# A small triangular inversion moved among the projections of r and v, affine steps on ScalarE, fillers given out anew

## The chip, the cores and the metric

One core of a Trainium2 chip runs one launch. The metric is the device time of that launch in microseconds (us). TensorE (PE) multiplies matrices, VectorE (DVE) and ScalarE (ACT) work elementwise, GpSimd (POOL) takes a few steps, and SyncE (SP) issues the loads.

## What is computed

Two layers over 256 positions of width 1024. A layer is a mixer and a feed-forward part (PEER), each followed by a LayerNorm. The mixer projects its input once, to the inputs of three branches and of their gates; the branches are a gated linear recurrence (RG-LRU), RWKV-7 and attention with low-rank latents (MLA). The change lies in the mixer, for the most part in RWKV-7:

```python
r, k, v, xw, xa, xg = split_last(p, (RW_WIDTH, RW_WIDTH, RW_WIDTH, LORA_W, LORA_A, LORA_G))
w = -jax.nn.softplus(-(w0 + jnp.tanh(xw) @ w2)) - 0.5
a = jax.nn.sigmoid(a0 + xa @ a2)
...
kk = hd(k * k_k).astype(jnp.float32)
kk = kk / jnp.maximum(jnp.sqrt(jnp.sum(kk * kk, -1, keepdims=True)), 1e-12)
k = k * (1.0 + (a - 1.0) * k_a)
decay = jnp.exp(-jnp.exp(w.astype(jnp.float32)))
...
xs = (tm(f32h(r)), tm(f32h(decay)), tm(f32h(k)), tm(f32h(v)), tm(-kk), tm(kk * a_h))
def step(state, inp):
    r_t, w_t, k_t, v_t, aa_t, bb_t = inp
    sa = jnp.einsum('bhvk,bhk->bhv', state, aa_t)
    state = (state * w_t[:, :, None, :] + sa[..., None] * bb_t[:, :, None, :]
             + v_t[..., None] * k_t[:, :, None, :])
    return state, jnp.einsum('bhvk,bhk->bhv', state, r_t)
```

The recurrence over 256 steps is computed in four chunks of 64 positions. In a chunk the delta rule needs the inverse of a triangular 64x64 matrix per head, whose entries are products of `kk` and `kk * a` with their decays. So there are 4 chunks x 8 heads = 32 such matrices in a layer.

## The kernel before, in words

**Projections.** All matrices are multiplied in a split form: `stream()` loads a 128x1024 weight tile (L82), ScalarE rounds it to `hi` (L84), VectorE subtracts to get `lo` (L88), and `projecting()` issues 24 matmuls for it (L247 to L249: hi times x-hi, hi times x-lo, lo times x-hi). It is a generator that yields every three matmuls, a *piece*. Each tile so needs one `lo` of VectorE before its third matmul.

**Fillers.** `rwkv_prep()` and `rwkv_scan()` are the main line. Beside them stands a list of generators: the latents and attention scores of MLA (`lat`), the projections of RG-LRU (`rgp`, `rgg`), the gates of branch 1 and the output products of branches 2 and 0. `fill(n, r)` takes n pieces from the front of that list, and before them up to r steps of the generator `rg_scan()`, once its inputs are there. Where the `fill` calls stand in the program, and with what n, sets what runs beside the main line; the scheduler then orders each engine's instructions by it.

**`rwkv_prep()`** projects the LoRA inputs and k, computes `at` and `sg` (L471 to L476), the head norms, then projects r and v, four tiles each with `fill(4)` behind each. After that come the gate, for layer 1 the value residual, the scan of the decays (`cum`, L542), its exponentials (L545 to L547), and two tiles per chunk, `AR` (with `kk` and r) and `KB` (with k and `kk * a`), L559 to L565. One set of matmuls per chunk gives all products of `KB` and `AR`; VectorE masks them into `GM` (L582).

**`rwkv_scan()`** inverts. POOL copies the diagonal 32x32 blocks of the triangles out of `GM` (`lu`, L602), VectorE transposes them (`lt`, L605) and runs 31 steps of substitution on all 64 blocks at once, a product (L613) and a sum (L615) each, each dependent on the one before: 62 instructions. L617 to L629 lay the result out (`tts`, `tp`, `t1s`, `t1u`, `TT`). `fill(124, 5)` stands behind as cover. Then TensorE joins the 32x32 blocks to 64x64 ones: eight groups of L638, which read `t1u`, eight more of L647, each with `fill(2)`. Then follows the scan over four chunks, in each four groups of small matmuls with `fill(4, 3)`, `fill(5, 3)` and `fill(2, 3)` between, and the group norm (L712). L310 in `head_bcast()` copies head statistics for a transposition, L463 scales k, L474 adds w0, L495 is an affine step of `at`, L729 the first tap of the convolution.

Of the kernel before, what the change touches and what calls it, by code (L numbers as in the profile page):

```python
# [45 lines left out]
def trunk(ctx, tc, x, xT, w_in, w_br, w_out, w_q, skT, uT, vt, prm, lora, g2, v1, v2, rgw, w_uq, w_ukv,  # L46
# [232 lines left out]
    def mixer(l, mp):  # L279
# [172 lines left out]
        def rwkv_prep():  # L452
            nonlocal la, k_, at, sg, r_, v_, g_, GM, VS, KS, AR, KB, pcm
# [29 lines left out]
            r_ = c4("r")  # L483
            for i in range(4):
                shifted(T_R + i, r_[:, i, :])
                fill(4)
            for b in range(2):
                V.tensor_mul(kk[:, :, b * P:(b + 1) * P], kk[:, :, b * P:(b + 1) * P], head_bcast(rs, b))
            v_ = c4("v")
            for i in range(4):  # L490
                shifted(T_V + i, v_[:, i, :])
                fill(4)
            t2 = c4("t2")
            for i in range(4):
                V.tensor_scalar(t2[:, i, :], at[:, i, :], ka[:, l, i:i + 1], ka[:, l, 4 + i:5 + i], op0=OP.mult, op1=OP.add)  # L495
# [42 lines left out]
            rmask = mp.tile([P, 1024], F32, tag="yt", name=nm("rmask"))
            G.memset(rmask, 1.0)
            G.memset(rmask[:, 0:1024:64], 0.0)  # L540
            cum, e1 = c4("t1"), c4("t2")
            V.tensor_tensor_scan(cum.rearrange("p i t -> p (i t)"), rmask,  # L542
                                 sg.rearrange("p i t -> p (i t)"), 0.0, op0=OP.mult, op1=OP.add)
            V.tensor_sub(sg, cum, sg)
            A.activation(e1, cum, AF.Exp, scale=-EXPM)  # L545
            A.activation(cum, cum, AF.Exp, scale=EXPM)
            A.activation(sg, sg, AF.Exp, scale=-EXPM)  # L547
            pcm = mp.tile([P, 4, 4, 2], F32, tag="pcm", name=nm("pcm"))
            e4 = e1.rearrange("p i (c t) -> p i c t", c=4)
            V.tensor_mul(pcm, e4[:, :, :, 63:64].to_broadcast([P, 4, 4, 2]),  # L550
                         bones[:, None, None, :].to_broadcast([P, 4, 4, 2]))
            AR = mp.tile([P, 4, 4, 2, 64], F32, tag="AR", name=nm("AR"))
            KB = mp.tile([P, 4, 4, 2, 64], F32, tag="KB", name=nm("KB"))

            def ch(t):
                return t.rearrange("p i (c t) -> p i c t", c=4)

            for i in range(4):
                V.tensor_mul(AR[:, i, :, 0, :], ch(kk)[:, i], ch(sg)[:, i])  # L559
# [647 lines left out]
```

## Time and profile before

| | us |
|---|---|
| Median of 3 runs | 2335.33 (2332.97 to 2336.89) |
| The profiled execution, its own time | 2339.72 |
| Its span in the profile | 2338.0 |
| TensorE busy in the span | 2242.7 |
| VectorE busy | 1790.2 |
| ScalarE busy | 1088.5 |
| GpSimd busy | 278.4 |

The profile's times count from the span's start. The mixer of layer 0 lies at about 10 to 345 us, that of layer 1 at about 1175 to 1510 us. Busy time of TensorE counts a matmul at half clock as twice as long, so a busy engine isn't one at its best; the granted clock stands beside it as a share of 2.4 GHz.

### The profile page before, as it was taken

Reading aid. Unit: us, or ns where it says so; the run is one execution under the profiler, and the core shown is the slowest. Engines: PE = TensorE matmul, PEld = TensorE weight load, DVE = VectorE, ACT = ScalarE, POOL = GpSimd, SP = SyncE. Lnnn points to the kernel's source line nnn. Section 1 sums busy time; section 2 is a strip of 40 time slices with the busy share of each in tenths; the row PEclk is TensorE's granted clock in tenths of the full one; section 3 lists DMA queues with packets and bytes.
Section 4 is the critical chain, followed back from the end, with each engine's and each line's share of the span. In section 5 each row is a group of like instructions: output and inputs, shape, how many; then the busy total and the mean of one; then the engine's idle time right before and its main releaser. Section 6 shows DMA issues by size and latency. Waiting matters only on the chain. (4 is left out here: it accounts for less than half of the span.)

```text
span 2338.0 us, 39856 instructions
## 1 busy us (share of the span) xinstructions
PE 2242.7 (96%) x15748; PEld 1980.1 (85%) x15748; DVE 1790.2 (77%) x3268; ACT 1088.5 (47%) x1635; POOL 278.4 (12%) x220
## 2 busy tenths in 40 slices
PE   7999989999999999999899999899999999999998
PEld 6888879998888888888787888799988888888886
DVE  6777877966788888755666877789668888887556
ACT  4543534445555544444445534344455555444443
POOL 0010016930000000000000100179300000000000
PEclk9998999999999999999999989999999999999999
DMA  6323344555555555655552234445555555556554
GB/s 212 118 79 113 133 164 146 165 184 185 175 170 172 173 176 170 213 196 190 189 174 91 91 109 134 160 142 170 183 184 177 172 171 172 174 171 214 194 193 136
DMA packets 104925, 381.88 MB, mean 163 GB/s; under 512 B 11649, under 2 KB 12161, under 8 KB 104481
## 3 DMA queue, kind: packets, MB, share of 16 engines
q1 hardware_dynamic: 104736, 379.32, 48.7%
q8 instruction: 124, 2.03, 0.3%
q14 instruction: 65, 0.52, 0.1%
HBM read 374.56 MB, written 4.72 MB: 162 GB/s over the span
## 5 line engine op out<-in xcount | busy, mean ns | idle before, releaser
L84 ACT CAST hi<-raw 128x1024 fp32r<-128x1024 f32 x658 | 690.3, 1050 | 756.2 <-PE acc L262 343.7
L88 DVE TENSOR_TENSOR lo<-raw,hi 128x1024 fp32r<-128x1024 f32 x570 | 696.0, 1222 | 250.0 <-ACT hi L84 242.5
L262 PE MATMUL acc<-hi,a 128*128 128x512 f32 x2000 | 554.6, 392 | 0.9 <-ACT a L166 0.9
L247 PE MATMUL mm<-xt,hi 128*128 128x256 f32 x1760 | 516.3, 294 | 23.7 <-ACT hi L84 11.7
L249 PE MATMUL mm<-xt,lo 128*128 128x256 f32 x1760 | 508.5, 290 | 13.9 <-DVE lo L88 10.5
L248 PE MATMUL mm<-xt,hi 128*128 128x256 f32 x1760 | 507.5, 288 | 0.0
L994 PE MATMUL acc<-xt,hi 128*128 128x512 f32 x1344 | 474.4, 399 | 0.0
L262 PEld LDWEIGHTS acc<-hi,a 128*128 128x128 f32 x2000 | 370.9, 188 | 76.2 <-ACT a L166 1.2
L247 PEld LDWEIGHTS mm<-xt,hi 128*128 128x128 f32 x1760 | 345.3, 196 | 31.0 <-ACT hi L84 11.7
L249 PEld LDWEIGHTS mm<-xt,lo 128*128 128x128 f32 x1760 | 344.3, 196 | 20.1 <-DVE lo L88 12.5
L997 PE MATMUL acc<-xt,lo 128*128 128x256 f32 x1344 | 348.7, 280 | 0.0
L248 PEld LDWEIGHTS mm<-xt,hi 128*128 128x128 f32 x1760 | 345.4, 196 | 2.1 <-issue 0.8
L262 PE MATMUL acc<-lo,a 128*128 128x512 f32 x1000 | 311.4, 391 | 0.0
L994 PEld LDWEIGHTS acc<-xt,hi 128*128 128x128 f32 x1344 | 245.4, 188 | 44.4
L88 POOL TENSOR_TENSOR lo<-raw,hi 128x512 fp32r<-128x512 f32 x176 | 251.5, 1455 | 244.9 <-ACT hi L84 243.2
L997 PEld LDWEIGHTS acc<-xt,lo 128*128 128x128 f32 x1344 | 253.5, 189 | 12.1
L262 PEld LDWEIGHTS acc<-lo,a 128*128 128x128 f32 x1000 | 187.7, 188 | 40.6 <-DVE lo L88 0.2
L1002 ACT COPY H<-acc 128x256 f32<-128x256 f32 x168 | 62.7, 373 | 232.0 <-PE acc L994 232.0
L1003 DVE TENSOR_TENSOR H<-H,acc 128x256 f32<-128x256 f32 x168 | 70.1, 417 | 60.8 <-ACT H L1002 60.8
L167 DVE SCALAR_TENSOR_TENSOR a<-H,a 128x1024 fp32r<-128x1024 f32 x64 | 78.4, 1225 | 44.7 <-ACT a L166 44.7
L166 ACT ACTIVATE a<-H 128x1024 fp32r<-128x1024 f32 x64 | 67.9, 1060 | 77.2 <-PE acc L262 76.9
L1094 DVE SCALAR_TENSOR_TENSOR H<-sm,H 128x512 f32<-128x512 f32 x128 | 87.7, 685 | 19.4 <-PE sm L1091 18.6
(356 smaller groups left out, 2381.4 us busy)
## 6 DMA issues: line engine op xcount, KB each, us to landing
raw<-in_uT_dram SPq DMA_DIRECT2D x256, 512.0 KB, 3.5
raw<-in_vt_dram SPq DMA_DIRECT2D x256, 512.0 KB, 3.8
raw<-in_w_in_dram SPq DMA_DIRECT2D x100, 512.0 KB, 3.5
raw<-in_w_q_dram SPq DMA_DIRECT2D x32, 512.0 KB, 3.5
raw<-in_w_br_dram SPq DMA_DIRECT2D x24, 512.0 KB, 3.6
raw<-in_w_out_dram SPq DMA_DIRECT2D x16, 512.0 KB, 4.1
ln<-in_lnp_dram SPq DMA_DIRECT2D x8, 512.0 KB, 4.9
xd<-ln SPq DMA_DIRECT2D x6, 512.0 KB, 2.6
```

The costliest lines, as they stand in the source:

```text
L84: A.copy(hi, raw)
L88: eng.tensor_sub(lo[:, c:c + n], raw[:, c:c + n], hi[:, c:c + n].bitcast(F32))
L166: A.activation(hi, src, AF.Copy, scale=scale)
L167: V.scalar_tensor_tensor(lo, src, scale, hi.bitcast(F32), op0=OP.mult, op1=OP.subtract)
L247: T.matmul(pt, h3[:, k, :], xth[:, k, :], start=(k == 0), stop=False)
L248: T.matmul(pt, h3[:, k, :], xtl[:, k, :], start=False, stop=False)
L249: T.matmul(pt, l3[:, k, :], xth[:, k, :], start=False, stop=(k == 7))
L262: T.matmul(acc[b][hf], m[:, bs], w[:, 512 * hf:512 * hf + 512], start=(k == 0 and j == 0), stop=(k == n - 1 and j == 2))
L994: T.matmul(p, h3[:, k, :], xt[:, k].rearrange("p a t -> p (a t)"), start=(k == 0), stop=(k == 7))
L997: T.matmul(p[:, 0:S], l3[:, k, :], xt[:, k, 0], start=False, stop=False)
L1003: V.tensor_add(h, h, p[:, 0:S])
L1094: V.scalar_tensor_tensor(hv, p.rearrange("p (t e) -> p e t", t=8), 1 / GATE_SCALE, hv, op0=OP.mult, op1=OP.mult)
```

## The change

- A new generator `ahead()` in `rwkv_prep()` holds the preparation of the decays, the halves of `AR` and `KB` that need neither r nor v, and the whole inversion. It makes the triangles by 32 small matmuls of its own (L530, 64x64) and 16 masked products (L535, 32x4x32) in place of the eight copies L602. It is stepped three times per projection of r and v, with `fill(2)` after two of these steps, and then to its end with `fill(2)` between.
- `rwkv_scan()` begins with the layout of the inverse. `fill(124, 5)` becomes `fill(28, 5)`, the sixteen `fill(2)` become `fill(4)`, and 4, 5 and 2 pieces per chunk become 9, 10 and 7.
- From VectorE to ScalarE go L310, L463, L474 (folded into the Tanh by a bias), L495, L712 and L729. L562 and L760 are folded into their neighbours' constants, L791 and L793 become one instruction.

```diff
             for i in range(4):
                 shifted(T_K + i, k_[:, i, :])
-                V.tensor_scalar(kk[:, i, :], k_[:, i, :], pcol(l, "k_k", i), None, op0=OP.mult)
+                A.activation(kk[:, i, :], k_[:, i, :], AF.Copy, scale=pcol(l, "k_k", i))
...
-                V.tensor_scalar(sg[:, i, :], p, pcol(l, "w0", i), None, op0=OP.add)
-            A.activation(sg, sg, AF.Tanh, scale=0.5)
+                A.activation(sg[:, i, :], p, AF.Tanh, bias=hb[:, l, 12 + i:13 + i], scale=0.5)
...
+            def ahead():
+                nonlocal cum, e4, ti, pcm
+                t2 = c4("t2")
+                for i in range(4):
+                    A.activation(t2[:, i, :], at[:, i, :], AF.Identity, bias=ka[:, l, 4 + i:5 + i], scale=ka[:, l, i:i + 1])
+                V.tensor_mul(k_, k_, t2)
+                yield
+                for b in range(2):
+                    V.tensor_mul(kk[:, :, b * P:(b + 1) * P], kk[:, :, b * P:(b + 1) * P], head_bcast(rs, b))
+                    yield
...
+                V.scalar_tensor_tensor(at, at, 1.0, kk, op0=OP.add, op1=OP.mult)
+                yield
+                for i in range(4):
+                    V.tensor_mul(AR[:, i, :, 0, :], ch(kk)[:, i], ch(sg)[:, i])
+                yield
+                for i in range(4):
+                    V.scalar_tensor_tensor(KB[:, i, :, 1, :], ch(at)[:, i], -0.5, ch(cum)[:, i], op0=OP.mult, op1=OP.mult)
+                yield
...
+                lu = mp.tile([P, 32, 32], F32, tag="sg", name=nm("lu"))
+                for c in range(4):
+                    for a in range(2):
+                        p = pacc()
+                        b = 64 * a
+                        for i in range(4):
+                            T.matmul(p[64:128, i * 64:(i + 1) * 64], KB[b:b + 64, i, c, 1, :], AR[b:b + 64, i, c, 0, :],
+                                     start=True, stop=True)
+                        pv = p[:, 0:256].rearrange("p (h t) -> p h t", h=4)
+                        for q in (0, 1):
+                            o = 64 + 32 * q
+                            V.tensor_mul(lu[o:o + 32, :, 8 * c + a:8 * c + 8:2].rearrange("p t u -> p u t"),
+                                         pv[o:o + 32, :, 32 * q:32 * q + 32],
+                                         gmask[o:o + 32, 0:1, 32 * q:32 * q + 32].to_broadcast([32, 4, 32]))
+                    yield
...
+                for s in range(31):
+                    n, m = 31 - s, s + 1
+                    tv = tmp[64:128, 0:n * m].rearrange("p (t j) -> p t j", t=n)
+                    V.tensor_mul(tv, lt[64:128, s + 1:32, s:s + 1].to_broadcast([64, n, m]),
+                                 ti[64:128, s:s + 1, 0:m].to_broadcast([64, n, m]))
+                    V.tensor_add(ti[64:128, s + 1:32, 0:m], ti[64:128, s + 1:32, 0:m], tv)
+                    if s % 2:
+                        yield
+
+            early = ahead()
+            r_, v_ = c4("r"), c4("v")
+            for t, dst in [(T_R + i, r_[:, i, :]) for i in range(4)] + [(T_V + i, v_[:, i, :]) for i in range(4)]:
+                next(early, None)
+                shifted(t, dst)
+                for _ in range(2):
+                    next(early, None)
+                    fill(2)
+            for _ in early:
+                fill(2)
...
-            fill(124, 5)
+            fill(28, 5)
...
-                    fill(2)
+                    fill(4)
...
-                fill(4, 3)
+                fill(9, 3)
...
-                fill(5, 3)
+                fill(10, 3)
...
-                fill(2, 3)
+                fill(7, 3)
```

In the order of the instructions this shows at three places. A row is a line, an operation, and out<-in with its shape; the same tile name has a new number in the changed kernel, and lines behind `ahead()` have moved.

The first is VectorE in layer 0, before: the end of the inversion in the scan (`ti` is the inverse being built, `lt` the triangles, `t1u` and `TT` its laid-out forms, `uu` the first result of TensorE that uses it).

```order
L615 TENSOR_TENSOR ti_1542<-ti_1542,tmp_1545 64x2x30
L613 TENSOR_TENSOR tmp_1545<-lt_1540,ti_1542 64x31
L615 TENSOR_TENSOR ti_1542<-ti_1542,tmp_1545 64x31
L617 STREAM_TRANSPOSE tts_1608<-ti_1542 64x1024
L619 COPY tp_1610<-ti_1542 32x1024
L629 COPY TT_1616<-tts_1608 32x16x32
L621 STREAM_TRANSPOSE t1s_1612<-tp_1610 32x1024
L629 COPY TT_1616<-tts_1608 32x16x32
L623 COPY t1u_1614<-t1s_1612 32x1024
L629 COPY TT_1617<-tts_1608 32x16x32 x2
L641 COPY uu_2137<-sm_2138 32x128
```
Every one of these rows hangs on the one before it, up to `t1u`, and L641 on TensorE's use of it. TensorE at the same place, where L835 to L837 are pieces of branch 2's output product, a filler:

```order
L836 MATMUL acc_2165<-ycl_1287,hi_2161 128x256
L837 MATMUL acc_2165<-ych_1286,lo_2163 128x256
L835 MATMUL acc_2191<-ych_1286,hi_2161 128x256
L638 MATMUL sm_2138<-t1u_1614,GM_1339 32x32 x4
L638 MATMUL sm_2150<-t1u_1614,GM_1339 32x32 x4
L836 MATMUL acc_2191<-ycl_1287,hi_2161 128x256
```
The first L638 so stands behind one filler tile that is under way. In the changed kernel the rows that read `t1u` (L662 now) stand among projections of a filler on TensorE:

```order
L249 MATMUL mm_1777<-xt_155,lo_1775 128x256
L247 MATMUL mm_1777<-xt_155,hi_1773 128x256
L248 MATMUL mm_1777<-xt_155,hi_1773 128x256
L249 MATMUL mm_1777<-xt_155,lo_1775 128x256
L662 MATMUL sm_1794<-t1u_1661,GM_1463 32x32 x4
L247 MATMUL mm_1777<-xt_155,hi_1773 128x256
L248 MATMUL mm_1777<-xt_155,hi_1773 128x256
```
The fillers round it are another tile's now. There `t1u` is written by VectorE 18 rows ahead of the `lo` of this projection; the rows between are fillers and `GM`:

```order
L647 COPY t1u_1661<-t1s_1659 32x1024
L755 SCALAR_TENSOR_TENSOR m_1452<-xp_1450,pr,m_1452 128x256
L430 RECIPROCAL amx_1356<-amx_1356 128x2
L653 COPY TT_1663<-tts_1655 32x16x32
L431 TENSOR_TENSOR pb_1359<-pb_1359,amx_1356 128x512
L653 COPY TT_1663<-tts_1655 32x16x32
L167 SCALAR_TENSOR_TENSOR ycl_1411<-sm_1430,ych_1410 128x256
L653 COPY TT_1664<-tts_1655 32x16x32 x2
L755 SCALAR_TENSOR_TENSOR m_1452<-xp_1450,pr,m_1452 128x256
L88 TENSOR_TENSOR lo_1689<-raw_1685,hi_1687 128x1024
L167 SCALAR_TENSOR_TENSOR ycl_1411<-sm_1439,ych_1410 128x256
L624 TENSOR_TENSOR GM_1463<-acc_1476,gmask 128x4x128
```
The inversion and its layout, which stood last in front of L641, are now ahead of `GM`.

The second place is the projections of r on VectorE in the changed kernel (`r` L289 is the projected r, `AR` and `KB` the operands, `lu` the triangles). Before, no row of this kind stood there.

```order
L512 SCALAR_TENSOR_TENSOR at_384<-at_384,kk_209 128x1024
L515 TENSOR_TENSOR AR_473<-kk_209,sg_385 128x4x64 x4
L289 SCALAR_TENSOR_TENSOR r_475<-mm_616,pr,r_475 128x255
L518 SCALAR_TENSOR_TENSOR KB_474<-at_384,t_553 128x4x64 x4
L542 MEMSET ti_776 64x1024
L535 TENSOR_TENSOR lu_666<-acc_667,gmask 32x4x32 x2
L535 TENSOR_TENSOR lu_666<-acc_674,gmask 32x4x32 x2
L535 TENSOR_TENSOR lu_666<-acc_687,gmask 32x4x32 x2
```
So each `lu` product waits for small matmuls of TensorE, and these for `AR` and `KB` of VectorE.

The third place is the attention scores (`acc` L422 masked scores, `amx` their maxima and sums, `pb` the probabilities; `tmp` and `ti` are the inversion, L549 and L551). VectorE before:

```order
L422 TENSOR_TENSOR acc_1082<-acc_1082,cmask 128x512
L393 TENSOR_TENSOR qT_605<-qT_605,cl_350 32x256
L424 TENSOR_REDUCE amx_1102<-acc_1082 128x4
L393 TENSOR_TENSOR qT_605<-qT_605,cl_350 32x256
L425 TENSOR_SCALAR amx_1102<-amx_1102 128x4
L626 MEMSET TT_1617 32x16x32
L422 TENSOR_TENSOR acc_1112<-acc_1112,cmask 128x512
L725 MEMSET xp_1326 128x4x3
L88 TENSOR_TENSOR lo_1333<-raw_1329,hi_1331 128x1024
L430 RECIPROCAL amx_1102<-amx_1102 128x4
L424 TENSOR_REDUCE amx_1124<-acc_1112 128x4
L431 TENSOR_TENSOR pb_1105<-pb_1105,amx_1102 128x512
```
The maxima, sums and products of a score tile stand close together there. VectorE now:

```order
L425 TENSOR_SCALAR amx_1226<-amx_1226 128x4
L422 TENSOR_TENSOR acc_1236<-acc_1236,cmask 128x512
L551 TENSOR_TENSOR ti_776<-ti_776,tmp_779 64x6x26
L424 TENSOR_REDUCE amx_1248<-acc_1236 128x4
L549 TENSOR_TENSOR tmp_779<-lt_774,ti_776 64x135
L430 RECIPROCAL amx_1226<-amx_1226 128x4
L425 TENSOR_SCALAR amx_1248<-amx_1248 128x4
L551 TENSOR_TENSOR ti_776<-ti_776,tmp_779 64x5x27
L431 TENSOR_TENSOR pb_1229<-pb_1229,amx_1226 128x512
L549 TENSOR_TENSOR tmp_779<-lt_774,ti_776 64x112
L749 MEMSET xp_1450 128x4x3
L88 TENSOR_TENSOR lo_1457<-raw_1453,hi_1455 128x1024
```
Since then an L549 or L551 lies between nearly all of them, and the `lo` behind them is later by as many rows. TensorE now, which reads `pb` in L405 and then the `lo` behind it:

```order
L247 MATMUL mm_1390<-xt_155,hi_1386 128x256
L248 MATMUL mm_1390<-xt_155,hi_1386 128x256
L405 MATMUL acc_1258<-ident,pb_1229 128x128 x4
L418 MATMUL acc_1264<-kT_650,qT_649 128x256 x2
L249 MATMUL mm_1459<-xt_155,lo_1457 128x256
L247 MATMUL mm_1459<-xt_155,hi_1455 128x256
```
L405 and this L249 are thus queued behind rows of the inversion.

## Rows read from the trace of the kernel before

**Rows 1.** The profile page, part 1: busy us, share of the span and instructions of each engine.

```profile
PE 2242.7 (96%) x15748; PEld 1980.1 (85%) x15748; DVE 1790.2 (77%) x3268; ACT 1088.5 (47%) x1635; POOL 278.4 (12%) x220
```

**Rows 2.** Waits of TensorE, layer 0 from 115 us on: total us, times, longest us.

```profile
PE mm L249 <- DVE lo L88: 5.7, 3, 2.0
PE sm L638 <- DVE t1u L623: 3.9, 1, 3.9
PE sm L662 <- DVE s L684: 1.5, 1, 1.5
```

**Rows 3.** The same view, layer 1 from 1280 us on.

```profile
PE sm L638 <- DVE t1u L623: 5.1, 1, 5.1
PE mm L249 <- DVE lo L88: 2.4, 2, 2.1
```

**Rows 4.** Timeline, layer 0: start us, length us, engine, line, [idle before <-releaser].

```profile
202.41 1.05 PE L638 MATMUL sm<-t1u,GM 32*32 32x32 f32 x16 [3.90 <-DVE t1u L623]
```

**Rows 5.** Stretches of layer 0: length, busy us of PE, PEld, DVE, ACT, POOL, clock, DMA.

```profile
45.30:115.00 69.70, 64.99 (x450) 58.79 (x449) 52.76 (x115) 36.93 (x81) 1.88 (x1) 0.98 0.37 120
...
158.70:198.50 39.80, 37.81 (x299) 37.42 (x299) 37.30 (x71) 15.68 (x23) 0.00 (x0) 0.96 0.52 171
...
202.40:216.00 13.60, 13.59 (x95) 11.43 (x96) 6.80 (x15) 1.52 (x2) 0.00 (x0) 0.50 0.23 78
216.00:266.00 50.00, 47.47 (x523) 43.04 (x523) 35.32 (x50) 23.36 (x35) 1.89 (x1) 0.97 0.29 96
266.00:302.00 36.00, 32.95 (x275) 31.89 (x274) 31.67 (x53) 16.36 (x22) 0.00 (x0) 0.95 0.57 189
```

**Rows 6.** The same view, stretches of layer 1.

```profile
1203.00:1280.00 77.00, 70.08 (x471) 60.62 (x469) 52.03 (x98) 39.47 (x72) 2.87 (x1) 0.98 0.31 103
...
1366.90:1379.90 13.00, 13.00 (x86) 10.31 (x87) 6.20 (x13) 2.00 (x3) 0.00 (x0) 0.50 0.20 61
...
1424.00:1434.50 10.50, 10.23 (x74) 9.47 (x73) 7.00 (x8) 1.66 (x2) 0.00 (x0) 0.51 0.61 205
1434.50:1470.00 35.50, 32.30 (x268) 31.45 (x265) 29.43 (x50) 17.22 (x24) 0.00 (x0) 0.95 0.54 175
```

**Rows 7.** VectorE's groups by line and shape, layer 0: busy us, mean ns of one, idle before.

```profile
L641 DVE COPY uu<-sm 32x128 f32<-32x128 f32 x8 | 2.3, 295 | 5.9 <-PE sm L638 5.9
...
L474 DVE TENSOR_SCALAR sg<-acc,pr 128x256 f32<-128x256 f32 x4 | 1.8, 480 | 0.9 <-PE acc L473 0.9
...
L310 DVE COPY hex<-hrs 128x512 f32<-128x512 f32 x4 | 1.7, 422 | 0.1
...
L495 DVE TENSOR_SCALAR t<-at,ka 128x256 f32<-128x256 f32 x4 | 1.5, 405 | 0.0
...
L605 DVE STREAM_TRANSPOSE lt<-lu 64x1024 f32<-64x1024 f32 x1 | 1.2, 1242 | 1.4 <-POOL lu L602 1.4
...
L615 DVE TENSOR_TENSOR ti<-ti,tmp 64x256 f32<-64x256 f32 x1 | 0.4, 423 | 0.0
...
L615 DVE TENSOR_TENSOR ti<-ti,tmp 64x31 f32<-64x31 f32 x2 | 0.4, 201 | 0.1
```

**Rows 8.** Timeline of VectorE, layer 0, where one line meets another.

```profile
98.61 0.42 DVE L561 TENSOR_TENSOR KB<-k,t 128x256 f32<-128x256 f32 x1
99.07 0.42 DVE L393 TENSOR_TENSOR qT<-qT,cl 32x256 f32<-32x256 f32 x1
99.41 0.41 DVE L390 TENSOR_TENSOR qT<-acc,rp 32x256 f32<-32x256 f32 x1
...
181.25 0.41 DVE L613 TENSOR_TENSOR tmp<-lt,ti 64x240 f32<-64x240 f32 x1
181.69 1.23 DVE L88 TENSOR_TENSOR lo<-raw,hi 128x1024 fp32r<-128x1024 f32 x1
```

**Rows 9.** Timeline, layer 1, TensorE: eight 64x64 matmuls, sixteen records.

```profile
1394.27 1.14 PE L668 MATMUL sm<-xs,TT 64*64 64x64 f32 x16
```

**Rows 10.** Waits of VectorE, layer 0, 45.3 to 115 us.

```profile
DVE lo L88 <- PE mm L249: 2.8, 1, 2.8
```

More of the change, by code (lines that the diff above doesn't have):

```diff
@@ L127, in trunk @@
     V.tensor_scalar(omm, pr[:, :, PC["mix"]:PC["mix"] + 14], -1.0, 1.0, op0=OP.mult, op1=OP.add)
-    hb = const.tile([P, L, 12], F32, tag="hb", name="hb")
-    for i, n in enumerate(("a0", "bx", "v0")):
+    hb = const.tile([P, L, 16], F32, tag="hb", name="hb")
+    for i, n in enumerate(("a0", "bx", "v0", "w0")):
         V.tensor_scalar(hb[:, :, 4 * i:4 * i + 4], pr[:, :, PC[n]:PC[n] + 4], 0.5, None, op0=OP.mult)
@@ L482, in rwkv_prep @@
             rsqrt(rs, st, 16)
-            r_ = c4("r")
-            for i in range(4):
[L485 to L495, printed above, removed]
@@ L496, in rwkv_prep, with ch @@
-            V.tensor_mul(k_, k_, t2)
+            rmask = mp.tile([P, 1024], F32, tag="yt", name=nm("rmask"))
+            G.memset(rmask, 1.0)
+            G.memset(rmask[:, 0:1024:64], 0.0)
+            AR = mp.tile([P, 4, 4, 2, 64], F32, tag="AR", name=nm("AR"))
+            KB = mp.tile([P, 4, 4, 2, 64], F32, tag="KB", name=nm("KB"))
+            cum = e4 = None
+            def ch(t):
+                return t.rearrange("p i (c t) -> p i c t", c=4)
+            def ahead():
[8 more added lines that the diff above has]
+                    yield
+                cum, e1 = c4("t1"), c4("t2")
+                V.tensor_tensor_scan(cum.rearrange("p i t -> p (i t)"), rmask,
+                                     sg.rearrange("p i t -> p (i t)"), 0.0, op0=OP.mult, op1=OP.add)
+                yield
+                V.tensor_sub(sg, cum, sg)
+                A.activation(sg, sg, AF.Exp, scale=-EXPM)
+                A.activation(e1, cum, AF.Exp, scale=-EXPM)
+                A.activation(cum, cum, AF.Exp, scale=EXPM)
+                yield
[7 more added lines that the diff above has]
+                yield
+                pcm = mp.tile([P, 4, 4, 2], F32, tag="pcm", name=nm("pcm"))
+                e4 = e1.rearrange("p i (c t) -> p i c t", c=4)
+                V.tensor_mul(pcm, e4[:, :, :, 63:64].to_broadcast([P, 4, 4, 2]),
+                             bones[:, None, None, :].to_broadcast([P, 4, 4, 2]))
+                lu = mp.tile([P, 32, 32], F32, tag="sg", name=nm("lu"))
[12 more added lines that the diff above has]
+                                         gmask[o:o + 32, 0:1, 32 * q:32 * q + 32].to_broadcast([32, 4, 32]))
+                    yield
+                lt = mp.tile([P, 32, 32], F32, tag="at", name=nm("lt"))
+                V.transpose(lt[64:128].rearrange("p t u -> p (t u)"), lu[64:128].rearrange("p t u -> p (t u)"))
+                ti = mp.tile([P, 32, 32], F32, tag="kk", name=nm("ti"))
+                V.memset(ti[64:128], 0.0)
+                V.memset(ti[64:128].rearrange("p t u -> p (t u)")[:, 0:1024:33], 1.0)
+                tmp = mp.tile([P, 32 * 32], F32, tag="sg", name=nm("tmp"))
+                yield
+                for s in range(31):
[5 more added lines that the diff above has]
+                    if s % 2:
+                        yield
@@ L536, in rwkv_prep @@
                 nc.sync.dma_start(vsave, v_)
[L538 to L559, printed above, removed]
-                V.tensor_mul(AR[:, i, :, 1, :], ch(r_)[:, i], e4[:, i])
-                V.tensor_mul(KB[:, i, :, 0, :], ch(k_)[:, i], ch(cum)[:, i])
-            V.tensor_scalar(at, at, -0.5, -0.5, op0=OP.mult, op1=OP.add)
-            V.tensor_mul(at, at, kk)
-            for i in range(4):
-                V.tensor_mul(KB[:, i, :, 1, :], ch(at)[:, i], ch(cum)[:, i])
             while fillers and fillers[0] is lat:
@@ L711, in rwkv_scan @@
             for i in range(4):
[L712 removed]
+                A.activation(yt[:, i, :], yt[:, i, :], AF.Identity, bias=pcol(l, "gn_b", i), scale=pcol(l, "gn_g", i))
             V.tensor_add(yt, yt, v_)
```

45 lines of the change are left out of this document (12 added, 33 removed).

## The prediction

> **What bounds the kernel now.** The page's first part comes first: TensorE is busy 96% of the span and VectorE 77% [rows 1]. So little can be gained except where TensorE stands still or runs at half its clock, and the change touches only the two mixers (about 10 to 345 us and 1175 to 1510 us). I therefore read TensorE's waits in the mixers [rows 2, 3], then the timeline round the longest of them [rows 4], then the same stretches with busy time and granted clock [rows 5, 6].
>
> In rows 2 and 3 the longest wait is L638's for `t1u`, the last tile of the inversion: 3.9 us in layer 0, 5.1 us in layer 1. The timeline shows what TensorE does then: nothing from 198.51 to 202.41 us, until VectorE's L623 has written the tile [rows 4]. In the 40 us before, VectorE is busy 37.3 of 39.8 us and TensorE 37.8 [rows 5]: the fillers meant to cover the inversion need VectorE too, a `lo` (L88) for each weight tile, and both engines end about together. After the wait the granted clock is 0.50 for 13.6 us in layer 0 and 13.0 us in layer 1 [rows 5, 6], which is 1.2 GHz instead of 2.4: the wait is paid a second time in clock.
>
> The r and v stretch, where the change puts the inversion, is 69.7 us with VectorE busy 52.8 in layer 0, and 77.0 with 52.0 in layer 1, while TensorE is busy 65.0 and 70.1 [rows 5, 6]. VectorE has room there of 16.9 and 25.0 us, but not in one piece.
>
> **The change, term by term.** Durations are from the profiled execution (2339.7 us, span 2338.0); it lies 4.4 us above the median of 2335.3, and I put the sum of differences on the median.
>
> *1. The wait for the inversion goes.* In the new order L662 (L638 before) stands among projections, dozens of VectorE rows behind `t1u`. Gone: 3.9 + 13.6 x 0.5 = 10.7 us in layer 0, and 5.1 + 13.0 x 0.5 = 11.6 us in layer 1 [rows 2, 3, 5, 6]. Sum -22.3. Next late there would be `GM` (L624), whose products stand right behind the inversion on VectorE; the projections lie between.
>
> *2. Smaller waits behind it shrink.* With 62 instructions less on VectorE, and 9, 10 and 7 pieces of filler instead of 4, 5 and 2 in each step of the scan, TensorE should seldom wait for `lo` (5.7 and 2.4 us) or, in layer 0, for L684 (1.5 us) [rows 2, 3]. The half-clock time there is one minus the granted clock times length: 39.8 x 0.04 + 50.0 x 0.03 + 36.0 x 0.05 = 4.9 us in layer 0, and 10.5 x 0.49 + 35.5 x 0.05 = 6.9 us in layer 1 [rows 5, 6]. Together 12.1 + 9.3 = 21.4 us. The later bursts (`lo` tiles at the last branch) aren't touched by the change, so between all and half I take three quarters: -16.1, ends -21.4 and -10.7.
>
> *3. The r and v stretch becomes VectorE's.* Up to the first scores that TensorE transposes (L405, which needs L431), VectorE gets 54 of the 62 inversion instructions. They run from 423 ns (64x256) to 201 ns (64x31) [rows 7]; the 62 of the trace add up to 21.1 us, less the last eight at 0.2 to 0.27 us, so 19.2, and each stands 0.03 us behind its predecessor, another 1.6. The 16 masked products (L535) are in no row; the nearest is L641, 32x128, at 0.295 us: 4.7. The transposition L605 comes in, 1.24. Three copies L310 go to ScalarE, -1.3 [rows 7]. So 52.8 + 19.2 + 1.6 + 4.7 + 1.2 - 1.3 = 78.2 us in layer 0, and 77.4 in layer 1.
>
> Alternation has a price too. Two neighbours without a dependence overlap a little if they lie on the same partitions: L393 runs from 99.07 to 99.49, and L390 starts at 99.41. If they don't, the second starts 0.03 us after the first has ended: L561 (128 rows) ends at 99.03, L393 (32 rows) starts at 99.07; L613 (64 rows) ends at 181.66, `lo` (128 rows) starts at 181.69 [rows 8]. So a switch costs 0.08 + 0.03 = 0.11 us against an overlapped pair. The new order switches from an inversion piece to another line 51 times before that L431; 16 of these are to L390 or L393, which stood apart from most of their neighbours before. I price the other 35: 3.9 us a layer. Without a price for switching the kernel would come out 7.8 us faster, at 2317. The Trainium skill, page VectorE: DVE Perf Modes, section on two Vector instructions with no wait between them, has a rule for this: an instruction whose operands start in another group of 32 partitions than those of the instructions before is held until all earlier ones have finished. Taken for all 51 switches it would make 5.6 us a layer and the sum 2328.
>
> Against that, VectorE starts the stretch earlier: L474 (1.8 us) and L495 (1.5 us) ahead of it go to ScalarE [rows 7]; I take 3.0. Need: 79.1 and 78.3 us. Not all idle time can be filled: I keep the 2.8 us in which `lo` waits for TensorE in layer 0 [rows 10], and 8 of 25 us in layer 1, where TensorE's own work is 4 to 5 us longer. The stretches become 81.9 and 86.3 us, +12.2 and +9.3: +21.5. TensorE isn't the limit there: the 32 new small matmuls, at 1.14 us for eight [rows 9], add 4.6 us, so it needs 69.6 and 74.7. Its new waits should lie at L530, at `lo`, and longest before L405, where L431 stands behind a row of inversion pieces. Ends: no idle left and no price for switching, +2.9; all idle kept, 79.1 + 16.9 - 69.7 and 78.3 + 25.0 - 77.0, +52.6.
>
> *4. Clock after the longest new wait.* Before, a wait of 3.9 us and more was followed by a half-speed stretch that cost 6.5 to 6.8 us [rows 2, 5, 6]. Two such stretches, one per layer, would cost 13, none 0; I take 6.5.
>
> *5. At nothing.* The affine steps on ScalarE (L463, L712, L729 too): it is busy 36.9 of 69.7 us in the r and v stretch [rows 5], so they fit; if a burst of them delays a `hi`, the `lo` behind it is late, and that is in term 3's idle. L602 leaves POOL, and L605 then waits for nobody. DMAs are the same in number; SP's queue holds the same loads in another order. L562, L760 and the merged L791 with L793 leave VectorE at places where it isn't last.
>
> Sum: -22.3 - 16.1 + 21.5 + 6.5 = -10.4, so 2335.3 - 10.4 = **2325**. With every term at its good end: -22.3 - 21.4 + 2.9 + 0 = -40.8 (2295); at its bad end: -22.3 - 10.7 + 52.6 + 13 = +32.6 (2368).
>
> **Rivals.**
> *A, slower: the clock.* Every new wait is followed by half speed: per layer one long stretch (6.65 us, the mean of 6.8 and 6.5) and four short ones at 1.6 us (the loss in the stretch before L638, 39.8 x 0.04 [rows 5]). That is 26.1 us instead of 6.5: +9.2, 2345. For it: at 1424 us of layer 1, 10.5 us ran at 0.51 [rows 6]. Against it: most new waits are short, and between them TensorE works. It decides from 22 us of clock loss on: then the kernel is slower by more than 0.2%, 4.7 us, about what a measurement of this kernel can tell from no change. The Trainium skill, page TensorE: Matmul & The Clock Gate, section HAM oscillation, tells of a kernel in which every wait between two bursts dropped the engine back to its lower level; by that rule this rival would hold.
>
> *B, no change: VectorE keeps stopping for others.* If a third of the idle that I let vanish stays (10.4 of 14.1 + 17.0 us), the gain is gone: 2335. For it: the r and v stretch has stops of VectorE for a `lo` whose raw tile or whose TensorE buffer is late [rows 10]; a piece of inversion fills it only if the order has one there.
>
> *C, a larger gain.* No idle is left (+9.4 and +1.3), term 2 goes whole and no stretch runs at half clock: -22.3 - 21.4 + 10.7 = -33.0, 2302. For it: a wait that TensorE has among projections may be filled by the piece behind.
>
> The change does what it says only in part: the inversion doesn't end among the projections of r and v, but runs on to the scores. Were all of it past them, term 3 would fall on the stretch behind; that is within B.
>
> **How the numbers follow.** Forecast 0.48 (alone 2312 to 2331), C 0.14, B 0.20, A 0.18. The range reaches to C and A: 2301 to 2345. Faster 0.62, same 0.20, slower 0.18.
>
> **What will show it.** Right: no wait for `t1u` at L662 and full clock there; VectorE busy over 93% from 44 us up to L405, that stretch 10 to 14 us longer; new TensorE waits at L530, `lo` and L405. Wrong: `t1u` still the longest wait (term 1); `lo` waits as large in the scan and after it (term 2); the r and v stretch no longer than before, or 20 us longer (term 3); several stretches at 0.50 in it (term 4, rival A).

## The result and the profile after

The changed kernel took 2317.69 us (median of 4 runs, 2316.89 to 2318.69) against 2336.11 of the kernel before; ratio 0.9922, 95% interval 0.9907 to 0.9936. That is 18.4 us less; 10.4 were forecast. The profiled execution took 2318.31 us.

The page's first part, which answers to [rows 1]:

```profile
PE 2232.0 (96%) x15876; PEld 1969.0 (85%) x15876; DVE 1774.9 (77%) x3243; ACT 1109.1 (48%) x1685; POOL 269.2 (12%) x204
```
TensorE's shares are as before, its busy time 10.7 us less and VectorE's 15.3. The mixers show where it went. TensorE's waits from the joins to the end of the mixer, layer 0 and then layer 1, answer to that part of [rows 2, 3]:

```profile
PE acc L262 <- DVE ml L167: 0.4, 1, 0.4
PE acc L262 <- ACT mh L166: 0.3, 1, 0.3
...
PE acc L262 <- DVE ml L167: 0.3, 1, 0.3
PE acc L262 <- ACT mh L166: 0.2, 1, 0.2
```
Nothing else is left behind the joins: no wait for `t1u`, none for `lo`, none for `s`. The same stretches in the view of [rows 5, 6] (length, busy us of PE, PEld, DVE, ACT, POOL, granted clock, DMA), layer 0 and then layer 1:

```profile
168.50:200.00 31.50, 31.50 (x321) 28.85 (x320) 16.14 (x28) 10.76 (x17) 0.00 (x0) 1.00 0.43 141
200.00:250.00 50.00, 50.00 (x531) 48.12 (x531) 36.77 (x47) 27.22 (x41) 1.89 (x1) 1.00 0.48 158
250.00:306.00 56.00, 56.00 (x491) 54.99 (x490) 44.12 (x73) 31.15 (x43) 0.00 (x0) 1.00 0.56 180
...
1325.00:1360.00 35.00, 35.00 (x348) 31.76 (x347) 18.11 (x31) 11.83 (x20) 0.00 (x0) 1.00 0.43 143
1360.00:1410.00 50.00, 50.00 (x538) 48.42 (x537) 36.93 (x46) 27.61 (x41) 1.89 (x1) 1.00 0.47 149
1410.00:1463.00 53.00, 53.00 (x459) 52.19 (x458) 42.70 (x71) 30.17 (x42) 0.00 (x0) 1.00 0.58 189
```
From the joins on TensorE is busy all the time at full clock, and VectorE isn't the limit: 16.1 of 31.5 us at the joins, where it had 37.3 of 39.8 ahead of them before.

The price is in the r and v stretch, in layer 0:

```profile
45.30:124.70 79.40, 68.16 (x502) 60.19 (x500) 73.94 (x177) 36.44 (x80) 2.94 (x1) 0.96 0.31 102
...
67.30:71.00 3.70, 0.03 (x1) 0.03 (x1) 3.48 (x9) 0.00 (x0) 0.00 (x0) 0.65 0.00 0
71.00:75.30 4.30, 4.30 (x20) 4.30 (x21) 3.99 (x14) 0.00 (x0) 0.00 (x0) 0.50 0.38 122
```
It is 79.4 us now up to the first L405, which stood at 113.1 us before: 11.6 us later. VectorE is busy 73.9 us of it. In the second row TensorE stands still for 3.7 us, and in the third it runs at half clock behind that. The timeline (start, length, engine, line) shows whom it waits for:

```profile
62.56 3.66 DVE L535 TENSOR_TENSOR lu<-acc,gmask 32x128 f32<-32x128 f32 x9 [1.33 <-PE acc L530]
66.25 0.48 DVE L289 SCALAR_TENSOR_TENSOR r<-mm,pr,r 128x255 f32<-128x255 f32 x1
66.77 2.72 DVE L535 TENSOR_TENSOR lu<-acc,gmask 32x128 f32<-32x128 f32 x7
...
69.69 1.23 DVE L88 TENSOR_TENSOR lo<-raw,hi 128x1024 fp32r<-128x1024 f32 x1
...
70.97 0.58 PE L249 MATMUL mm<-xt,lo 128*128 128x256 f32 x1 [3.68 <-DVE lo L88]
```
All sixteen masked products of the triangles stand on VectorE ahead of the `lo` of the next projection. In layer 1 the same wait is 3.7 us, and a second one at the scores, L405 for `amx` (2.3 us), is followed by half clock too. The waits of TensorE there:

```profile
PE mm L249 <- DVE lo L88: 6.0, 4, 3.7
PE acc L405 <- DVE amx L425: 2.8, 2, 2.3
```
and the two stretches behind the long ones, in the columns of [rows 5]; the clock is 0.50 for 6.8 us in all at the first, from inside the wait on, and for 10.3 us behind the second:

```profile
1217.70:1222.10 4.40, 4.40 (x21) 4.40 (x22) 4.06 (x16) 0.00 (x0) 0.00 (x1) 0.50 0.35 119
...
1297.20:1307.50 10.30, 10.23 (x52) 7.94 (x51) 6.94 (x12) 2.57 (x6) 1.91 (x4) 0.50 0.17 52
```
A balance of the two mixers, worked out from the traces: the length of each mixer up to the 8.4 us wait in its last LayerNorm (L210), TensorE's idle stretches over 0.02 us, its time at the lower clock (half of it counted as lost), and the rest, which holds the idle time at the mixer's start too. In us, layer 0 / layer 1, of one profiled execution each, here and of the experiments below:

| kernel | length | idle | at half clock | rest |
|---|---|---|---|---|
| before | 332.7 / 346.8 | 21.9 / 21.5 | 27.3 / 44.4 | 297.2 / 303.1 |
| changed | 320.6 / 336.1 | 16.6 / 15.5 | 6.8 / 27.3 | 300.6 / 307.0 |
| E1 moves | 331.2 / 333.1 | 17.1 / 15.5 | 37.5 / 27.3 | 295.3 / 304.0 |
| E6 inversion | 331.6 / 344.4 | 21.6 / 19.1 | 17.1 / 27.3 | 301.5 / 311.6 |
| E7 eight pieces | 320.7 / 328.8 | 14.0 / 13.1 | 10.2 / 17.1 | 301.6 / 307.2 |
| E12 rest in GM | 319.1 / 329.2 | 13.2 / 10.3 | 6.8 / 20.5 | 302.6 / 308.6 |

The change takes 12.1 + 10.7 = 22.8 us off the mixers of the profiled executions: 11.3 of idle time, 18.8 of clock, and 7.3 us more of the rest. The clock's share is rough. Some half-clock time lies in idle stretches (0.4 / 6.7 us before, 2.5 / 7.7 changed). And the profiled execution of before has a mean granted clock of 0.979, where its other runs on record have 0.980 to 0.984, so a few us of the 18.8 are that execution's own. Kernels with the inversion moved have a rest 3 to 9 us a layer higher than before; the 32 new matmuls, 3.7 us in layer 0 of the changed kernel, are the larger part where it is 4.

### The profile page after: what moved, and what is told of

The parts are those of the page before. It is cut to its first block, busy times and chain, and to the rows that moved or that the text cites. A ratio compares the mean times of both kernels' runs of the same rounds, so it can differ in the third digit from the quotient of the medians.

```text
span 2316.5 us, 40125 instructions
## 1 busy us (share of the span) xinstructions
PE 2232.0 (96%) x15876; PEld 1969.0 (85%) x15876; DVE 1774.9 (77%) x3243; ACT 1109.1 (48%) x1685; POOL 269.2 (12%) x204
## 4 chain that ended last, share of the span: by engine, by line
PE 88%; DVE 7%; issue 2%; ACT 1%; DMA 1%; POOL 1%; SPq 0%; DVEq 0%; POOLq 0%; ACTq 0%
PE acc L262 32%; PE acc L1014 14%; PE mm L247 8%; PE mm L249 8%; PE mm L248 8%; PE acc L1017 7%; PE sm L1111 3%; DVE lo L88 1%; PE acc L855 1%; PE acc L857 1%; PE acc L856 1%; POOL lo L88 1%; PE sm L982 1%; PE acc L622 1%; DVE tmp L549 1%
## 5 line engine op out<-in xcount | busy, mean ns | idle before, releaser
L247 PE MATMUL mm<-xt,hi 128*128 128x256 f32 x1760 | 514.0, 292 | 19.3 <-ACT hi L84 11.9
L249 PE MATMUL mm<-xt,lo 128*128 128x256 f32 x1760 | 505.3, 288 | 17.9 <-DVE lo L88 14.2
L247 PEld LDWEIGHTS mm<-xt,hi 128*128 128x128 f32 x1760 | 341.6, 194 | 27.1 <-ACT hi L84 11.9
L249 PEld LDWEIGHTS mm<-xt,lo 128*128 128x128 f32 x1760 | 341.0, 194 | 25.5 <-DVE lo L88 17.9
L248 PEld LDWEIGHTS mm<-xt,hi 128*128 128x128 f32 x1760 | 341.7, 194 | 1.5 <-DVE xt L167 0.7
L1014 PEld LDWEIGHTS acc<-xt,hi 128*128 128x128 f32 x1344 | 245.4, 188 | 44.4
L1017 PEld LDWEIGHTS acc<-xt,lo 128*128 128x128 f32 x1344 | 253.5, 189 | 12.1
L166 ACT ACTIVATE a<-H 128x1024 fp32r<-128x1024 f32 x64 | 67.8, 1060 | 76.9 <-PE acc L262 76.6
```

The lines of the kernel that those rows point to most:

```text
L247: T.matmul(pt, h3[:, k, :], xth[:, k, :], start=(k == 0), stop=False)
L248: T.matmul(pt, h3[:, k, :], xtl[:, k, :], start=False, stop=False)
L249: T.matmul(pt, l3[:, k, :], xth[:, k, :], start=False, stop=(k == 7))
L1014: T.matmul(p, h3[:, k, :], xt[:, k].rearrange("p a t -> p (a t)"), start=(k == 0), stop=(k == 7))
L1017: T.matmul(p[:, 0:S], l3[:, k, :], xt[:, k, 0], start=False, stop=False)
```

## The experiments

The change has three parts: the move of the inversion, the moved and folded affine steps, the new fills. My theory was that the first brings the gain and the others help. The rivals were that the lighter VectorE, or the fills, bring it. Six kernels fill the table of combinations, one cell of it not cleanly. The median of before differs by up to 2.8 us between the sets of runs, so each kernel's ratio to the runs of before taken with it is what counts; differences in us against the changed kernel are of medians and carry that drift.

**E1, the affine moves alone.** Three of the edits to the kernel before:

```diff
-                V.tensor_scalar(kk[:, i, :], k_[:, i, :], pcol(l, "k_k", i), None, op0=OP.mult)
+                A.activation(kk[:, i, :], k_[:, i, :], AF.Copy, scale=pcol(l, "k_k", i))
...
-                V.tensor_scalar(yt[:, i, :], yt[:, i, :], pcol(l, "gn_g", i), pcol(l, "gn_b", i), op0=OP.mult, op1=OP.add)
+                A.activation(yt[:, i, :], yt[:, i, :], AF.Identity, bias=pcol(l, "gn_b", i), scale=pcol(l, "gn_g", i))
...
-            V.tensor_scalar(rt, rt, 0.5, None, op0=OP.mult)
```

> The kernel before with only the steps moved from VectorE to ScalarE and the folded constants; the inversion and the fills stay. Theory (the gain is the wait for the inversion and what followed it): of the 8 us less per mixer on VectorE little lies in the 40 us before L638, so the wait for t1u stays at 3 to 5 us per layer with its half-clock stretch; -2 to -6 us against before, 2330 to 2334. Rival (the lighter VectorE is the gain): -12 us or more, and the wait for t1u under 1.5 us.

Measured: 2324.07 us, ratio 0.9946 (0.9929 to 0.9962). TensorE's waits, layer 0 and layer 1:

```profile
PE sm L636 <- DVE t1u L621: 4.8, 1, 4.8
...
PE sm L636 <- DVE t1u L621: 4.9, 1, 4.9
...
PE mm L249 <- DVE lo L88: 0.5, 2, 0.3
```
Both were half right. The wait for `t1u` is as long as before, as I expected; the gain is 10.7 us, where I expected 2 to 6. What shrinks are the other waits: of 2.4 us for `lo` in layer 1 [rows 3] 0.5 is left.

**E9, only L712, L729, L760 and L791 with L793** (told here since it splits E1; L729 begins at 127 us, ahead of the inversion, and runs into it; the others stand behind it):

```diff
-                V.tensor_scalar(yt[:, i, :], yt[:, i, :], pcol(l, "gn_g", i), pcol(l, "gn_b", i), op0=OP.mult, op1=OP.add)
+                A.activation(yt[:, i, :], yt[:, i, :], AF.Identity, bias=pcol(l, "gn_b", i), scale=pcol(l, "gn_g", i))
...
-            V.tensor_scalar(g3, g3, 0.044715, 1.0, op0=OP.mult, op1=OP.add)
...
-            V.tensor_mul(g3, g3, gx)
+            V.scalar_tensor_tensor(g3, g3, 1.0, gx, op0=OP.add, op1=OP.mult)
```

> The kernel before with only those steps moved or folded that run in the scan and behind it: L712 and L729 to ScalarE, L760, L791 and L793 folded; L310, L463, L474, L495 and L562 stay on VectorE. The run of all moves gave 10.7 us. Theory (the moves pay in the scan and at its end, where lo and L684 came late on VectorE): 6 to 11 us faster than before, 2324 to 2329, with the waits of 1.5 us at L662 and 2 us at L249 near the end of the mixer gone. Rival (they pay ahead of the inversion): within 4 us of before and those waits still there.

Measured: 2323.68 us, ratio 0.9957 (0.9944 to 0.9970), most of E1's gain. In its trace the wait for `lo` near the end of the mixer is gone in both layers; that at L662, 1.5 us in either layer before, is 0.6 us in layer 0, and 1.3 in layer 1:

```profile
PE sm L662 <- DVE s L684: 0.6, 1, 0.6
...
PE sm L662 <- DVE s L684: 1.3, 1, 1.3
```
That trace is of the run with the lowest time. The eight lie between 2315.52 us, at a mean granted clock of 0.985, and 2328.53 us, at 0.980.

**E6, the move of the inversion alone.** The changed kernel with the affine steps back, the constants of L760, L791 and L793 unfolded (that of L562 stays folded), and the old fills:

```diff
-                A.activation(yt[:, i, :], yt[:, i, :], AF.Identity, bias=pcol(l, "gn_b", i), scale=pcol(l, "gn_g", i))
+                V.tensor_scalar(yt[:, i, :], yt[:, i, :], pcol(l, "gn_g", i), pcol(l, "gn_b", i), op0=OP.mult, op1=OP.add)
...
-            fill(28, 5)
+            fill(124, 5)
```

> The changed kernel with the affine steps back on VectorE, the constants of L760, L791 and L793 unfolded and the fills of before: the move of the inversion alone. Theory one (the wait for t1u with its clock, 22 us, against the new waits in the r and v stretch, about 20): 2 to 8 us faster than before, 2327 to 2333, and the late lo waits of before still there. Theory two (the move adds nothing or costs): at or above 2334.

Measured: 2336.07 us, ratio 1.0001 (0.9991 to 1.0012). TensorE's waits, layer 0 from 168 us on, then the r and v stretch:

```profile
PE mm L249 <- DVE lo L88: 2.1, 1, 2.1
PE sm L687 <- DVE s L709: 1.5, 1, 1.5
PE acc L862 <- DVE lo L88: 0.8, 1, 0.8
...
PE mm L247 <- DVE cl L347: 3.3, 1, 3.3
PE mm L249 <- DVE lo L88: 2.1, 2, 1.7
PE mm L247 <- DVE r L289: 1.8, 3, 0.7
```
No wait for `t1u`; but behind the joins the waits stay: 1.5 us for `s` as before, and 2.1 for one `lo`, where the longest was 2.0 [rows 2]. So the inversion's place has nothing to do with these two. What the move gives back at the joins goes into new waits in the r and v stretch and into the higher rest (E6 in the table above).

**E3, the new fills alone**, and **E5, fills and moves**, both with the inversion still in the scan:

```diff
-            fill(124, 5)
+            fill(28, 5)
...
-                    fill(2)
+                    fill(4)
...
-                fill(4, 3)
+                fill(9, 3)
```

> The kernel before with the new fills, its inversion still in the scan, covered by 28 pieces instead of 124. 28 pieces of three matmuls at 0.12 us are 10 us, the inversion and its layout take VectorE about 28 us alone. Theory: TensorE waits 15 to 25 us for t1u in each layer and runs at half clock behind it; later waits are fewer; 20 to 50 us slower than before. Rival (the fills are the gain): faster than before by 5 us or more.

> The kernel before with the affine moves and the new fills, the inversion still in the scan: the changed kernel without its first part. Runs so far: moves alone 10.7 us faster than before, fills alone 6.3, both with the inversion moved 17. Theory one (moving the inversion is worth what it was between the run of the fills alone and the run with the affine steps back, 7 us): 2322 to 2326, with waits for lo in front of the joins and behind them. Theory two (the move of the inversion adds nothing, the moves and fills are all): within 3 us of the changed kernel, 2315 to 2321.

Measured: E3 2328.45 us, ratio 0.9976 (0.9964 to 0.9987); E5 2327.27 us, 0.9970 (0.9957 to 0.9983). E3's size was wrong: I had TensorE wait 15 to 25 us for `t1u`, it waits 0.9 and 2.2 us. The number in `fill` isn't the cover: from the first step of the inversion to the copy of `t1u` TensorE runs 395 matmuls in layer 0 and 340 in layer 1 (365 and 319 before), where 28 pieces are 84. The inversion doesn't end earlier for that: `t1u` is done at 208.8 us in layer 0, at 202.4 before, with fifteen `lo` in between in both. Waits for `lo` and `hi` (3.4 and 2.6 us in layer 0) come instead. E5's waits for `t1u` are 2.6 and 3.9 us, and behind them TensorE is at half clock for 24 us in either layer, though busy for most of it (columns of [rows 5]):

```profile
210.20:234.10 23.90, 22.55 (x162) 19.19 (x163) 11.46 (x25) 4.82 (x5) 0.00 (x0) 0.50 0.28 89
1367.40:1391.20 23.80, 22.22 (x185) 18.93 (x186) 15.31 (x29) 6.10 (x6) 0.00 (x0) 0.50 0.22 69
```
Theory two for E5 fell: it isn't within 3 us of the changed kernel. Theory one had the sign; the time lies 1.3 us above its range.

**E2, inversion and moves with the old fills**, and **E4, inversion and fills with the affine steps back**:

> The changed kernel with the fills of before in the scan (124, 2 and 4, 5, 2). Theory: no wait for t1u, but the scan's chunks are covered by fewer pieces again, so that short waits at the scan's steps and at lo behind it come back with some half clock: 4 to 12 us slower than the changed kernel, 2322 to 2330. Rival one (the inversion's place alone is the gain, the fills nothing): within 3 us of the changed kernel. Rival two (the fills are the gain): at or above 2334.

> The changed kernel with L310, L463, L474, L495, L712 and L729 back on VectorE (the folded constants stay). Theory: VectorE is the limit only in the r and v stretch, where 1.3 us of these lie, and 4.7 us lie just ahead of it; 2 to 8 us slower than the changed kernel, 2320 to 2326. Rival (the lighter VectorE is the gain): 12 us or more slower.

Measured: E2 2326.09 us, ratio 0.9953 (0.9936 to 0.9969); E4 2321.75 us, 0.9936 (0.9920 to 0.9953). E2 came out 8.4 us above the changed kernel (0.31% by the ratios), as expected in size, but not by its mechanism: the longest waits behind its joins are 0.6 us. E4 lies in its range, 4.1 us above the changed kernel, with overlapping intervals. Neither `s` nor `lo` keeps TensorE waiting behind its joins; a `hi` does, at 295 us in layer 0:

```profile
PE acc L856 <- ACT hi L84: 3.9, 1, 3.9
```
The table of ratios:

| | inversion in the scan | inversion moved |
|---|---|---|
| nothing else | 1 | 1.0001 |
| new fills | 0.9976 | 0.9936 |
| affine moves | 0.9946 | 0.9953 |
| both | 0.9970 | 0.9922 |

The cell that isn't clean is 0.9936: E4 keeps all folded constants (L562, L760, L791 with L793), E6 only that of L562, E3 none. A kernel with the inversion moved, the new fills and nothing else wasn't run.

With the old fills the move of the inversion is worth nothing, with or without the affine moves; with the new fills and the affine moves it is worth 0.5%, and 0.4% without the steps on ScalarE, the folded constants included. The fills by themselves gain 0.24%. Beside the affine moves they gain 0.31% where the inversion is moved, and cost 0.24% where it isn't, though the two intervals of each pair just meet. So the gain of the change isn't that of the inversion by itself. The affine moves alone give 0.54%, and beside them inversion and fills pay only together, another 0.24%, where again the intervals overlap a little. The parts don't add up: without the six steps on ScalarE the change already has 0.64 of its 0.78% (E4). E1, E9 and E4 have the folded constants of L760, L791 and L793 in common; what these bring alone wasn't tried.

**E7, the triangles in eight pieces.** This tests the price of the clump of sixteen products, by a yield for each of the two head parities:

```diff
                                          gmask[o:o + 32, 0:1, 32 * q:32 * q + 32].to_broadcast([32, 4, 32]))
-                    yield
+                        yield
```

> The changed kernel with a yield after every head parity of the triangles (eight pieces of two masked products) instead of four. In the order the lo of the next projection then stands ahead of the sixteen products L535 on VectorE. Theory (the 3.7 us wait for that lo and the half-clock stretch behind it, about 7 us a layer, are the price of the clump): that wait under 1 us and no stretch at 0.50 behind it; 8 to 14 us faster than the changed kernel, 2304 to 2310. Rival (VectorE is the limit there, the wait only goes elsewhere): within 4 us of it.

Measured: 2310.39 us, ratio 0.9893 (0.9873 to 0.9914), 7.3 us below the changed kernel, where the theory had 8 to 14. The `lo` now stands in front of the products (at 60.23 us, the first product at 62.59), the wait of 3.7 us is gone, and the longest ones left are at the scores:

```profile
PE acc L405 <- DVE pb L431: 2.8, 2, 2.2
...
PE mm L249 <- DVE lo L88: 1.3, 2, 0.7
...
PE acc L405 <- ACT pb L428: 4.2, 1, 4.2
```
But the balance above doesn't bear the theory out in layer 0. That mixer takes 320.7 us, 320.6 in the changed kernel, although the wait is gone: at L405, at L247 for `v` and at L578 for `la` waits of 0.9, 0.6 and 0.5 us have grown to 2.2, 2.0 and 2.0, as the rival has it. The gain stands in layer 1, 7.3 us, 5.1 of them clock.

**E8, the inversion only behind v:**

```diff
-                next(early, None)
                 shifted(t, dst)
-                for _ in range(2):
-                    next(early, None)
-                    fill(2)
+                fill(4)
```

> The changed kernel with fill(4) behind each projection of r and v, as before, and the generator of the inversion run only after v, with fill(2) between. Theory (VectorE had 17 and 25 us of room in the r and v stretch and 13 us in the one behind it): the 27 us of triangles and inversion now crowd the stretch with the scores and GM; TensorE waits there for lo and amx 10 us and more a layer; 5 to 20 us slower than the changed kernel. Rival (the place among r and v doesn't matter): within 3 us.

Measured: 2338.67 us, ratio 1.0020 (1.0007 to 1.0033), 21 us above the changed kernel, where 5 to 20 were expected. The place among r and v matters; but the wait that shows is for `t1u` again, not for `amx`:

```profile
PE sm L659 <- DVE t1u L644: 3.3, 1, 3.3
...
PE sm L659 <- DVE t1u L644: 4.3, 1, 4.3
```
**E10, E11 and E12** move what is left of the inversion behind v, all with eight pieces: fill(1), fill(3), or four steps left for the loop that makes `GM`:

```diff
-            for _ in early:
+            for _ in range(4):
+                next(early, None)
                 fill(2)
...
                 g, vs, ks = GM[c], VS[c], KS[c]
-                fill(3)
+                fill(2)
+                next(early, None)
+                fill(1)
+                if c == 3:
+                    drain(early)
```

> The kernel with eight triangle pieces, the rest of the inversion behind v with fill(1) between instead of fill(2). It still waits 2.2 us (layer 0) and 4.2 us (layer 1) at L405 for scores that stand between inversion pieces on VectorE. Theory (those waits come from the alternation with the scores): the inversion ends earlier among the scores, the waits get shorter: 1 to 5 us faster than with fill(2), 2305 to 2309. Rival (VectorE is the limit there whatever the order): within 2 us of 2310.

> The same with fill(3): inversion pieces spread further through the scores. Theory: more score tiles stand behind an inversion piece, but fewer pieces stand before the first; between 3 us faster and 3 us slower than with fill(2), 2307 to 2313. Rival (VectorE is the limit whatever the order): within 2 us of 2310.

> The same with four of the remaining inversion pieces left for the loop that makes GM, one per chunk and what is left in the last. Theory (the waits at L405 come from the inversion between the scores, and behind the scores TensorE needs nothing of it for 30 us): shorter waits at L405, 1 to 5 us faster than 2310. Rival (the pieces then delay GM and the joins): a wait for t1u or GM, 2 us or more slower than 2310.

Measured: E10 2311.92 us, ratio 0.9906 (0.9886 to 0.9925); E11 2313.34, 0.9913 (0.9895 to 0.9930); E12 2304.98, 0.9871 (0.9852 to 0.9889). The first two can't be told from E7 by their intervals, so the theory for E10 isn't borne out. E12 has the lowest median of all, but its interval overlaps E7's, so a gain over E7 isn't shown. Its waits at L405 are down as expected (layer 0, layer 1):

```profile
PE acc L405 <- ACT pb L428: 1.0, 1, 1.0
...
PE acc L405 <- DVE amx L430: 0.5, 1, 0.5
...
PE acc L405 <- DVE amx L425: 0.6, 1, 0.6
```
## Why the prediction was right, and where it wasn't

The time lay inside the forecast's own range, 7 us below its number. By its steps:

*Term 1, the wait for `t1u` (-22.3):* right. Both waits and both half-clock stretches behind are gone.

*Term 2, the waits behind it (-16.1):* too small, and right in cause for a part only. All 21.4 us went; I had taken three quarters. The failed step is "With 62 instructions less on VectorE". Of the 5.7 us for `lo` in layer 0 [rows 2] two waits stand ahead of the joins, while the inversion runs, and one near the end of the mixer; in TensorE's timeline of before:

```profile
158.65 0.39 PE L249 MATMUL mm<-xt,lo 128*128 128x256 f32 x1 [1.72 <-DVE lo L88]
...
163.77 0.38 PE L249 MATMUL mm<-xt,lo 128*128 128x256 f32 x1 [1.99 <-DVE lo L88]
...
297.31 0.39 PE L249 MATMUL mm<-xt,lo 128*128 128x256 f32 x1 [1.95 <-DVE lo L88]
```
E6 has the 62 instructions gone. It has lost the first two waits and keeps the third, and that for `s`. E9 has the instructions where they were. It has lost the third wait, still waits 1.1 and 0.4 us in place of the first two, and 0.6 for `s`. So behind the joins the step is wrong: what ends the last wait there is in term 5, which I set at nothing, as L712 fits on ScalarE and the folded steps "leave VectorE at places where it isn't last". In the trace of before L712 runs from 286.08 us in an almost unbroken row of VectorE instructions that ends with the late `lo` at 296:

```profile
286.08 1.38 DVE L712 TENSOR_SCALAR yt<-yt,pr 128x256 f32<-128x256 f32 x4
...
296.04 2.35 DVE L88 TENSOR_TENSOR lo<-raw,hi 128x1024 fp32r<-128x1024 f32 x2
```
For `s` the cause stays open. L760, L791 and L793 stand at 237 to 245 us, in the scan ahead of L684, but VectorE is idle 1.96 and 0.93 us between, and the late L684 at 259 us stands behind a long instruction of another branch (L784) that E9 has in the same place. Which step does how much wasn't tried.

*Term 3, the r and v stretch (+21.5):* its ends held within 2.5 us: the stretch takes 79.4 us in layer 0, 81.9 forecast, and 84.3 in layer 1, 86.3 forecast (counted from the same distance behind the LayerNorm before it). But the rows that I started from end at 115 and 1280 us, and the first L405 stood at 113.1 and 1285.4. So the stretch was 67.8 and 82.4 us long before, not 69.7 and 77.0, and grew by 11.6 us in layer 0 (12.2 forecast) and by 1.9 in layer 1 (9.3 forecast), where VectorE had been busy 57.0 of 82.4 us; waits among the later scores came instead. In layer 0 VectorE was busy 93%, as written. L535 took 383 ns and not 295, 1.4 us more a layer. The price of switching shows: in the changed kernel the median distance from the end of an inversion piece to the next instruction of another line is 0.03 us, against -0.08 us between two others, over 51 and 16 pairs of layer 0. That the time met 2317, the figure without this price, is chance.

*Term 4, the clock (+6.5):* near in the sum. 6.8 and 17.1 us at half clock between r and the joins make 12.0 us; before lost 5.1 us there too, at 66, 1250 and 1281 us, which stood in no term, so 6.9 are new. I had priced one stretch of 6.5; what came is 1.7 us in layer 0 and 5.1 in layer 1. The longest new wait in layer 0 isn't at L405, as I wrote, but at the `lo` behind L535.

Terms 1 and 2 in full are -43.7. The mixers of the profiled executions are 22.8 us shorter, so the new price is about 20.9 us, against 28.0 for terms 3 and 4; with 6.9 of clock in it term 3 came to 14.0 and not 21.5. The two errors, 5.3 and 7.1 us, have the same sign and add up; that the medians differ by 18.4 only is mostly because the profiled execution of before lay 3.6 us above its runs' median. Rival A had its mechanism (at each 3.7 us wait there is a half-speed stretch) but not its number. Rival B fell, with VectorE busy 93%. Rival C's 2302 was out of reach for the change, and E12 came near it. That the move pays nothing without the fills, and the fills cost time beside the affine moves without the move, was in none of my cases. What the new fills do for the moved inversion stays open: from E2 to the changed kernel a balance like the one above gives 3.4 us of clock, 2.4 of idle time and 3.3 of rest.

## What to carry to other kernels

Before a gain is put down to the large part of a change, ask which small step stands directly in front of the late tile: here a few short steps in and behind the scan, moved or folded, were worth 0.4% by themselves, and the long chain moved out of the way nothing by itself. Work moved into another engine's idle time should come in small pieces: sixteen products in a row cost a 3.7 us wait in either layer. But look where the time goes when the wait is gone: splitting them took 7.3 us off one mixer and nothing off the other, where other waits grew. And test the parts in combination, with every small step clearly in or out: here the move was worth nothing without the fills, and the fills cost time beside the affine moves without the move.
